# Pad tiles that bring TensorE's operands to one address modulo 256, and a start without GpSimd

## The chip, the cores and the metric

The kernel runs on one core of a Trainium2 chip. The metric is the device time of one execution in microseconds. Times of stretches come from one profiled execution and are counted from the start of its span.

## The reference

A two-layer diffusion backbone with D = 2048, 256 latent tokens and 256 context tokens, all in float32. Layer 0 mixes tokens with a windowed attention (16 heads of 128) that also sees the context; layer 1 mixes them with a gated MLP that multiplies 128-position chunks by a 128x128 matrix for each channel group. Each mixer is followed by a SwiGLU of inner width 5632. Shift, scale and gate of every sub-layer come from the conditioning vectors.

```python
for i in range(DEPTH):                       # DEPTH = 2
    sh1, sc1, g1, sh2, sc2, g2 = ada_params(c, ada_w[i], ada_b[i])   # silu(c) @ w + b
    a = modulate(h, sh1, sc1)
    y = na_mixer(a, ac, ...) if i == 0 else spatial_gating_mlp(a, ...)
    h = layer_norm(ALPHA * h + g1 * y, ...)
    h = layer_norm(ALPHA * h + g2 * swiglu(modulate(h, sh2, sc2), ffn_w_in[i], ffn_w_out[i]), ...)
```

## The kernel before

**Products.** Every large product is float32 split into two `float32r` halves, hi and lo, and made of three matmuls (`mm3`, L88 to L91): hi x hi, hi x lo, lo x hi. In `T.matmul(out, stationary, moving)` the second argument is loaded into the array by a weight load (PEld in the profile), the third streams through it; the profile names them `out<-moving,stationary`. One matmul streams 512 columns.

**Weights.** A queue of weight pieces of 128x1024 (`enqueue`, `prefetch`, `piece`) is loaded by SP into `raw` buffers and split by ScalarE (L94, hi) and VectorE (L95, lo). In layer 0's first half the split halves lie in three buffer pairs `hiA`, `loA` of the pool `outer`. From L553 on, five pairs are used in turn: of each five pieces three go to the `A` pairs in `outer` and two to the `B` pairs in the pool `main`. The last two pieces of some products go to `extra` tiles outside this turn.

```python
if pos["wide"] is not None and m % 5 > 2:
    pool, tag, bufs = pos["wide"], "B", 2
else:
    pool, tag, bufs = outer, "A", 3
```

**Input products** (`block_T`: the SwiGLU's gate and up, `pg` and `pu`, and the gated MLP's `gv` and `gu`) use tiles of the pool `main` as stationary operand: `f0h`, `f0l`, `m1h`, `m1l`, `f1h`, `f1l` (tags `acth`, `actl`). A piece gives 12 matmuls. **Output products** (`project_out`: `powo`, `pod`, `pogo`) use tiles `gh`, `gl` of `outer` (or `e`, also in `outer`). A piece gives 12 matmuls here too. In the attention half both operands lie in `outer`, `attnX`, `attnA` and `attnB`; a piece of `proj_v` gives 24 matmuls.

**Addresses.** A tile starts at a multiple of 32 bytes, and a pool's tags follow each other in the order of their first use; a pool opened later lies behind. In `outer` all tiles from `xT` on are whole multiples of 256 bytes, so `A`, `gh`, `gl`, `xT`, `ada` and the first tile of the pool behind, `ah` or `h`, have the same address modulo 256; call it r. In `main` follow `h` (16384 bytes), `ca` and `cb` (four of 64), `st` (two of 192): that is 128 past a multiple of 256, and `B`, `tmp`, `acth` and `actl` lie at r + 128. `mv` and `rs` (four of 32) bring `zt`, and the pools behind `main`, back to r. In the pool `gm` the 64 bytes of `bs` put `vv` at r + 64. The tiles `ah`, `al`, `kh`, `qh` and `v` of the attention half are at r.

**The start.** TensorE computes the first shift and scale columns with small matmuls (`dot`, L343: batches of 32 over a 1 MB load `ap`), a batch for each of two vectors, then `gather(kt)` (a ScalarE copy, L352, and two small matmuls against `sel`, L355; `sel` is a reduction of the identity, L314). `make_identity` builds the identity on GpSimd. After `gather(0)` two rows of the conditioning (`c_bc`, and `cc_bc`, which lies in `oT`) are each loaded to one partition by SP, spread over 128 partitions by GpSimd (`spread`, L81) and passed through SiLU by ScalarE (L382). From kt = 3 on VectorE uses them (L330). TensorE's order here is fixed by `pin`. Then the loop over kt: nine matmuls `kps`, the `dot` of kt + 2, twelve matmuls `vps`, `gather` of kt + 2, and from kt = 3 twelve matmuls `eps`.

**GpSimd later** zeroes the gate tiles (L171), spreads LayerNorm rows (L83) and sums the gates over partitions (`partition_all_reduce`, L192).

Of the kernel before, what the change touches and what calls it, by code (L numbers as in the profile page):

```python
# [11 lines left out]

F32 = mybir.dt.float32
F32R = mybir.dt.float32r
BF16 = mybir.dt.bfloat16
AF = mybir.ActivationFunctionType
# [4 lines left out]
P = 128  # L21
# [31 lines left out]
def hybrid_kernel(ctx: ExitStack, tc: tile.TileContext, i, out):  # L53
    nc = tc.nc
    V, S, T = nc.vector, nc.scalar, nc.tensor

    outer = ctx.enter_context(tc.tile_pool(name="outer", bufs=1))
# [3 lines left out]
    badj = outer.tile([P, 2, 6, KT], F32, tag="badj", name="badj")  # L61
    nc.scalar.dma_start(badj, i["ada_b_col"])
    ident = outer.tile([P, P], F32, tag="ident", name="ident")
    make_identity(nc, ident)
    eps_t = outer.tile([P, 1], F32, tag="eps", name="eps_t")
    nc.gpsimd.memset(eps_t, EPS)
    warm = outer.tile([P, 1], F32, tag="warm", name="warm")
# [13 lines left out]
    def spread(dst, src):  # L81
        nc.sync.dma_start(dst[0:1, :], src[None, :])
        nc.gpsimd.partition_broadcast(dst, dst[0:1, :])  # L83
# [194 lines left out]
    with tc.tile_pool(name="attnX", bufs=1) as px, ExitStack() as late:  # L278
# [21 lines left out]
        with tc.tile_pool(name="st", bufs=1) as st:  # L300
# [3 lines left out]
            def load_st(src, name, n):  # L304
# [2 lines left out]
                nc.sync.dma_start(r, src)  # L307
                return r

            c_pad = st.tile([P, KT, 32], F32, tag="cpad", name="c_pad")  # L310
            nc.gpsimd.memset(c_pad, 0.0)
            V.tensor_copy(c_pad[:, :, 0:2], c_col)
# [4 lines left out]
            vps = [stp_pool.tile([P, 512], F32, tag=f"v{b}", name=f"vps{b}") for b in range(4)]  # L317
            xt = {}
            c_bc = outer.tile([P, D], F32, tag="cbc", name="c_bc")
            cc_bc = oT[:, 0 : D // NT, :].rearrange("p a b -> p (a b)")  # L320
# [42 lines left out]
            def modulate(kt):  # L363
# [6 lines left out]
                    )  # L370
                split_into(ah[:, kt, :], al[:, kt, :], tmp)

            for kt in range(2):
                for t in range(2):
                    dot(kt, t)
                load_x(kt)
                prefetch(1)
                gather(kt)
                if kt == 0:
                    for n, bc in enumerate((c_bc, cc_bc)):  # L380
                        spread(bc, i["c_rows"][n])
                        S.activation(bc, bc, AF.Silu)  # L382
            modulate(0)
            for kt in range(KT):
                hi, lo = piece()
# [166 lines left out]
    main = ctx.enter_context(tc.tile_pool(name="main", bufs=1))  # L552
    pos["wide"] = main  # L553
    pos["bufs"] = 5
    h_t = main.tile([P, 2, D], F32, tag="h", name="h_t")
    nc.sync.dma_start(h_t, i["x_tok"])

    def act_tiles(name):
# [5 lines left out]
    def stats_tile(name):  # L564
        return main.tile([P, 2, NB, 6], F32, tag="st", name=f"st{name}", bufs=2)
# [96 lines left out]
    def project_out(kts, src, key, name, finish, extra, last=False):  # L662
        st = stats_tile(name)
        hold = LAST if last else HOLD
        for nh in range(2):
            if nh == 0:
                ps = [[acc_tile(f"po{name}{nh}{n}{b}") for b in range(2)] for n in range(2)]
            else:
                ps = [[s_tile(f"po{name}{nh}0{b}") for b in range(2)]]
                ps.append([acc_tile(f"po{name}{nh}1{b}") for b in range(2)])  # L670

            def products(kt, x, w, n, b):
                c, tb = slice(n * 512, (n + 1) * 512), slice(b * P, (b + 1) * P)
                mm3(ps[n][b], x[0][:, tb], x[1][:, tb], w[0][:, c], w[1][:, c], kt == 0, kt == kts - 1)

            def fetch(kt, n):
                xs = []
                for k in range(n):
                    at = None
                    if k >= START:  # L680
                        if k % 2 == 0:
                            e = outer.tile([P, 4, NT], F32R, tag="ada", name=f"e{name}{k}", bufs=ADA)
                        at = e[:, 2 * (k % 2), :], e[:, 2 * (k % 2) + 1, :]
                    xs.append(act_split(src(kt + k), f"{name}{nh}_{kt + k}", at))
                return xs, take(n)

            k0 = 0
            if nh == 1:
                xs, ws = fetch(0, START)
                for n in range(2):  # L690
                    for j in range(START):
                        for b in range(2):
                            products(j, xs[j], ws[j], n, b)
                preload_sqrt(st)
                k0 = START
            k1 = kts - hold if nh == 1 else kts
            for kt in range(k0, k1):
                if nh == 1 and kt == max(k1 - 9, k0):
                    pos["extra"] = extra()
                w = piece() if nh == 0 or kt < k1 - START else take(1)[0]  # L700
                x = act_split(src(kt), f"{name}{nh}_{kt}")
                for n in range(2):
                    for b in range(2):
                        products(kt, x, w, n, b)
                if nh == 0 or kt < k1 - QUIET:
                    tick()
            if nh == 0:
                need(key)
                g = gate[key]
                for n in range(2):  # L710
                    for b in range(2):
                        residual(ps[n][b], b, n, g, st, name)
            else:
                xs, ws = fetch(k1, hold)
                for b in range(2):
                    for n in range(2):
                        for j in range(hold):
                            products(k1 + j, xs[j], ws[j], n, b)
                        with tc.high_priority(AHEAD):
                            residual(ps[n][b], b, 2 + n, g, st, name)  # L720
                    if not last:
                        with tc.high_priority(AHEAD):
                            finish(b, st)
                if last:
                    for b in range(2):
                        finish(b, st)
# [25 lines left out]
    def ffn(layer, m, key, name, finish, free, last=False):  # L752
# [41 lines left out]
    m = Modulated(0, 0, SH2, SC2, "f0")  # L794
    free = ExitStack()
    pw = free.enter_context(tc.tile_pool(name="pw", bufs=1))
    project_out(
        KT, lambda k: oT[:, k, :], (0, G1), "wo", m.first,
        lambda: pw.tile([P, 4, 1024], F32R, tag="w", name="extra_o"),
# [21 lines left out]
    pg = free.enter_context(tc.tile_pool(name="gm", bufs=1))  # L821
    ws = pg.tile([P, NH, P], F32, tag="ws", name="ws")
    nc.sync.dma_start(ws, i["w_s"])
    bs = pg.tile([P, NH], F32, tag="bs", name="bs")
    nc.sync.dma_start(bs, i["b_s"])
    vv = pg.tile([P, 2, D], F32, tag="vv", name="vv")
    st = stats_tile("v")
    for nb in range(NB):
        ps = [acc_tile(f"gv{nb}{b}") for b in range(2)]
        block_T(m, ps, nb == 0)  # L830
        for b in range(2):
            sl = slice(nb * 512, (nb + 1) * 512)
# [106 lines left out]
def lay_out(x, c, ctx, c_ctx, ada_w, ada_b, ln_g, ln_b, na_w_qkv, na_w_o, na_rpb,  # L939
            gm_w_in, gm_ln_g, gm_ln_b, gm_w_s, gm_b_s, gm_w_out, ffn_w_in, ffn_w_out):  # L940
    a = {}
    x, ctx = x[0], ctx[0]
    rows = np.stack([c[0], c_ctx])
    a["c_rows"] = rows
    a["c_col"] = rows.reshape(2, KT, P).transpose(2, 1, 0)
    xc = np.concatenate([x, ctx], 0)
    a["xcT"] = xc.T.reshape(KT, P, 512)
    a["x_tok"] = x.reshape(2, P, D).transpose(1, 0, 2)
    a["ada_b_col"] = ada_b.reshape(2, 6, KT, P).transpose(3, 0, 1, 2)
    a["ada_b_row"] = ada_b.reshape(2, 6, D)  # L950
    g4, b4 = ln_g.reshape(4, D), ln_b.reshape(4, D)
    a["ln_row"] = np.stack([g4, b4], 1)
    a["ln_col"] = a["ln_row"].reshape(4, 2, KT, P).transpose(3, 0, 1, 2)
    aw = ada_w.reshape(2, D, 6, D)
    dot = np.empty((len(DOT), P, D), np.float32)
    for (layer, t, nt), n in DOT.items():
        dot[n] = aw[layer, :, t, nt * P : (nt + 1) * P].T
    a["ada_t"] = dot
    a["ada_g"] = np.concatenate(
        [aw[layer, :, t, :].reshape(KT, P, D) for layer in range(2) for t in (G1, G2)], 0  # L960
    )
    a["ada_p"] = np.stack(
        [[aw[0, :, t, kt * P : (kt + 1) * P].reshape(KT, P, P).transpose(1, 0, 2).reshape(P, 2048)
          for t in (SC1, SH1)] for kt in range(KT)]
    )
    a["ada_s"] = np.stack([aw[0, :, SH1, kt * P : (kt + 1) * P].T for kt in range(DVE0, KT)])
    wq, wk, wv = (na_w_qkv[0][:, n * D : (n + 1) * D] for n in range(3))
    w0 = np.concatenate([wk[:, : HK0 * P], wv[:, :512]], 1)
    a["w_kv0"] = w0.reshape(KT, P, W0)

    a["w_q"] = heads(wq)
    a["w_k"] = heads(wk)[HK0:]
    a["w_v"] = blocks_512(wv)[1:]
    a["bias"] = bias_layout(na_rpb[0])
    a["w_o"] = halves(na_w_o[0])
    parts = ffn_w_in.reshape(2, D, 2, DFF)
    a["w_in_t"] = np.stack([[blocks_512(parts[n, :, p]) for p in range(2)] for n in range(2)])
    a["w_out"] = np.stack([halves(w) for w in ffn_w_out])
    a["w_gin"] = blocks_512(gm_w_in[0])
    a["w_gout"] = halves(gm_w_out[0])  # L980
    a["gm_row"] = np.stack([gm_ln_g[0], gm_ln_b[0]])
    a["w_s"] = gm_w_s[0].transpose(2, 0, 1)
    a["b_s"] = gm_b_s[0].T
    return {k: np.ascontiguousarray(v) for k, v in a.items()}
# [17 lines left out]
```

## Time and profile before

| | before |
|---|---|
| median of 3 runs (lowest to highest) | 2493.1 us (2491.81 to 2497.22) |
| profiled execution: its time, its span | 2484.16 us, 2482.4 us |
| TensorE busy in the span | 2409.0 us, 97% |
| VectorE, ScalarE, GpSimd busy | 1754.9, 1118.9, 110.5 us |

A busy TensorE is not a TensorE at its best: a matmul counts as busy from its start to its modelled end, and matmuls overlap. How fast it goes is read from one start to the next.

### The profile page before, as it was taken

The numbers are of one execution on the slowest core, as the hardware profiler recorded it, in microseconds if no ns is written. First come the engines' busy times: TensorE is split into PE (matmuls) and PEld (weight loads), VectorE is DVE, ScalarE is ACT, GpSimd is POOL, SyncE is SP. The second block draws the span as 40 slices with busy tenths as digits, with TensorE's granted clock in tenths as the row PEclk, the third lists the DMA queues.
The fourth block names the chain that finished last, engine by engine and source line by source line (L and its number), as shares of the span: only waits on it lengthen the run. The fifth ranks groups of instructions, "written<-read, shape, count | busy, mean of one in ns | idle before, by whom it ended". The sixth has DMA issues, their size and how long they took to land. (4 is left out here: it accounts for less than half of the span.)

```text
span 2482.4 us, 31276 instructions
## 1 busy us (share of the span) xinstructions
PE 2409.0 (97%) x11574; PEld 1976.3 (80%) x11574; DVE 1754.9 (71%) x2159; ACT 1118.9 (45%) x1534; POOL 110.5 (4%) x56
## 2 busy tenths in 40 slices
PE   6999899999999999999999999999999999999998
PEld 5787788888778888888888778777888888888886
DVE  3878877776877676666778778778755555566666
ACT  3344434345554444444455554446544444445453
POOL 0000200000010020000000020020100000020000
PEclk8999999999999999999999999999999999999999
DMA  8977787777568878888888767765676666666563
GB/s 328 347 258 253 243 285 269 268 269 240 184 225 299 283 272 287 280 285 291 283 290 278 255 211 259 255 205 184 214 228 224 218 222 226 220 196 190 174 208 131
DMA packets 167394, 610.57 MB, mean 246 GB/s; under 512 B 18916, under 2 KB 21284, under 8 KB 162884
## 3 DMA queue, kind: packets, MB, share of 16 engines
q1 hardware_dynamic: 120888, 440.64, 53.5%
q10 hardware_dynamic: 46224, 167.89, 19.6%
q8 instruction: 90, 1.47, 0.2%
q14 instruction: 64, 0.52, 0.1%
q0 software_dynamic: 128, 0.03, 0.0%
HBM read 606.40 MB, written 2.10 MB: 245 GB/s over the span
## 5 line engine op out<-in xcount | busy, mean ns | idle before, releaser
L94 ACT CAST hwf<-rwf 128x1024 fp32r<-128x1024 f32 x320 | 335.7, 1049 | 505.6 <-PE pu L91 228.5
L95 DVE TENSOR_TENSOR lwf<-rwf,hwf 128x1024 fp32r<-128x1024 f32 x320 | 405.5, 1276 | 194.2 <-ACT hwf L94 193.3
L153 DVE SCALAR_TENSOR_TENSOR ad<-ad,c_bc 128x1024 f32<-128x1024 f32 x192 | 234.0, 1222 | 169.8 <-DMA ad<-in_ada_t 169.2
L91 PE MATMUL pod<-hwd,gld 128*128 128x512 f32 x684 | 267.9, 392 | 0.7 <-DVE gld L95 0.7
L89 PE MATMUL pod<-hwd,ghd 128*128 128x512 f32 x684 | 268.2, 392 | 0.0
L90 PE MATMUL pod<-lwd,ghd 128*128 128x512 f32 x684 | 267.8, 392 | 0.0
L95 DVE TENSOR_TENSOR lwd<-rwd,hwd 128x1024 fp32r<-128x1024 f32 x172 | 211.5, 1231 | 52.4 <-ACT hwd L94 51.9
L177 DVE SCALAR_TENSOR_TENSOR gate<-ag,c_col,gate 128x1024 f32<-128x1024 f32 x128 | 164.3, 1287 | 108.8 <-DMA ag<-in_ada_g 108.5
L94 ACT CAST hwd<-rwd 128x1024 fp32r<-128x1024 f32 x172 | 179.9, 1046 | 26.2 <-PE pu L91 17.2
L91 PEld LDWEIGHTS pod<-hwd,gld 128*128 128x128 f32 x684 | 128.3, 188 | 29.6 <-DVE gld L95 1.1
L90 PEld LDWEIGHTS pod<-lwd,ghd 128*128 128x128 f32 x684 | 128.4, 188 | 28.5
L89 PEld LDWEIGHTS pod<-hwd,ghd 128*128 128x128 f32 x684 | 128.4, 188 | 28.5
L89 PE MATMUL pg<-hwf,f0h 128*128 128x512 f32 x320 | 127.5, 398 | 0.0
L89 PE MATMUL pg<-hwf,f1h 128*128 128x512 f32 x320 | 127.5, 398 | 0.0
L91 PE MATMUL pg<-hwf,f1l 128*128 128x512 f32 x320 | 125.8, 393 | 0.0
L91 PE MATMUL pg<-hwf,f0l 128*128 128x512 f32 x320 | 125.8, 393 | 0.0
L90 PE MATMUL pg<-lwf,f0h 128*128 128x512 f32 x320 | 125.7, 393 | 0.0
L90 PE MATMUL pg<-lwf,f1h 128*128 128x512 f32 x320 | 125.7, 393 | 0.0
L91 PE MATMUL pu<-hwf,f0l 128*128 128x512 f32 x320 | 125.7, 393 | 0.0
L91 PE MATMUL pu<-hwf,f1l 128*128 128x512 f32 x320 | 125.7, 393 | 0.0
L90 PE MATMUL pu<-lwf,f0h 128*128 128x512 f32 x320 | 125.7, 393 | 0.0
L89 PE MATMUL pu<-hwf,f1h 128*128 128x512 f32 x320 | 125.7, 393 | 0.0
(341 smaller groups left out, 5341.9 us busy)
## 6 DMA issues: line engine op xcount, KB each, us to landing
rwf<-in_w_in_t SPq DMA_DIRECT2D x320, 512.0 KB
ad<-in_ada_t ACTq DMA_DIRECT2D x192, 512.0 KB
rwd<-in_w_out SPq DMA_DIRECT2D x176, 512.0 KB
ag<-in_ada_g ACTq DMA_DIRECT2D x128, 512.0 KB
rwg<-in_w_gin SPq DMA_DIRECT2D x64, 512.0 KB
ap<-in_ada_p SPq DMA_DIRECT2D x19, 1024.0 KB
rwq<-in_w_q SPq DMA_DIRECT2D x32, 512.0 KB
rwo<-in_w_o SPq DMA_DIRECT2D x32, 512.0 KB
```

What stands on the lines that cost most here:

```text
L89: keep(T.matmul(ps, sh, mh, start=first, stop=False))
L90: keep(T.matmul(ps, sh, ml, start=False, stop=False))
L91: keep(T.matmul(ps, sl, mh, start=False, stop=last))
L94: S.copy(hi, src)
L95: V.tensor_tensor(lo, src, hi.bitcast(F32), ALU.subtract)
L153: V.scalar_tensor_tensor(r, r, 1.0, c_bc[:, half * 1024 : (half + 1) * 1024], ALU.mult, ALU.mult, accum_out=o[:, nt : nt + 1],)
L177: V.scalar_tensor_tensor(g, loaded.pop(key), c_col[:, kt, 0:1], g, ALU.mult, ALU.add)
```

## The change

A tile of 32 floats (128 bytes) is put behind `h` in `main`, one of 128 bytes ahead of the `extra_o` tile in `pw`, and one of 64 bytes behind `bs` in `gm`. Nothing reads or writes them. The identity comes from DRAM over ScalarE's DMA queue instead of `make_identity`. The two conditioning rows are loaded, over the same queue, as two tiles of 2 partitions x 1024 in `loA` buffers; `pick` (in a `gh` buffer) holds a row of the identity's first two rows spread over 128 columns, and `widen` multiplies it with the rows, so that each of 4 matmuls gives 512 columns of one conditioning row on all 128 partitions, in the PSUM tiles `vps`. ScalarE takes SiLU from there. `widen(0)` stands ahead of the first `dot`, `widen(1)` behind `gather(0)`. The SP loads, GpSimd broadcasts and 2048-wide SiLUs of before are gone.

```diff
     ident = outer.tile([P, P], F32, tag="ident", name="ident")
-    make_identity(nc, ident)
+    nc.scalar.dma_start(ident, i["ident"])
...
+            c_row = [outer.tile([2, 1024], F32, tag="loA", name=f"c_row{e}", bufs=3) for e in range(2)]
+            for e in range(2):
+                nc.scalar.dma_start(c_row[e], i["c_rows"][:, e * 1024 : (e + 1) * 1024])
+            pick = outer.tile([2, 2, P], F32, tag="gh", name="pick", bufs=4)
+            for n in range(2):
+                V.tensor_copy(pick[:, n, :], ident[0:2, n : n + 1].to_broadcast([2, P]))
...
+            def widen(n, bc):
+                for q in range(4):
+                    sl = slice(q * 512, (q + 1) * 512)
+                    cs = slice(q % 2 * 512, q % 2 * 512 + 512)
+                    pin(T.matmul(vps[q], pick[:, n, :], c_row[q // 2][:, cs], start=True, stop=True))
+                    S.activation(bc[:, sl], vps[q], AF.Silu)
+
+            widen(0, c_bc)
             for kt in range(2):
                 for t in range(2):
                     dot(kt, t)
...
                 gather(kt)
                 if kt == 0:
-                    for n, bc in enumerate((c_bc, cc_bc)):
-                        spread(bc, i["c_rows"][n])
-                        S.activation(bc, bc, AF.Silu)
+                    widen(1, cc_bc)
...
     h_t = main.tile([P, 2, D], F32, tag="h", name="h_t")
+    main.tile([P, 32], F32, tag="pad", name="pad_main")
...
     pw = free.enter_context(tc.tile_pool(name="pw", bufs=1))
+    pw.tile([P, 32], F32, tag="pad", name="pad_pw")
...
     nc.sync.dma_start(bs, i["b_s"])
+    pg.tile([P, 16], F32, tag="pad", name="pad_gm")
     vv = pg.tile([P, 2, D], F32, tag="vv", name="vv")
...
+    a["ident"] = np.eye(P, dtype=np.float32)
```

## Rows read from the trace of the kernel before

**Rows 1.** The page's first part: busy us of each engine (share of the span) and its instructions.

```profile
PE 2409.0 (97%) x11574; PEld 1976.3 (80%) x11574; DVE 1754.9 (71%) x2159; ACT 1118.9 (45%) x1534; POOL 110.5 (4%) x56
```

**Rows 2.** Busy time by stretch. Columns: from:to, length, busy us and instruction count of PE, PEld, DVE, ACT and POOL, granted clock of PE, mean busy share of the DMA engines, GB/s.

```profile
72.00:150.00 78.00, 78.00 (x593) 62.11 (x592) 66.22 (x88) 30.19 (x54) 0.00 (x0) 1.00 0.91 331
150.00:600.00 450.00, 429.19 (x2366) 371.63 (x2365) 347.10 (x518) 190.19 (x309) 15.43 (x3) 0.98 0.78 261
600.00:1750.00 1150.00, 1130.71 (x4978) 915.21 (x4977) 864.64 (x1054) 555.97 (x745) 61.57 (x33) 1.00 0.76 256
1750.00:2450.00 700.00, 700.00 (x3086) 571.00 (x3085) 420.60 (x420) 314.45 (x385) 27.85 (x10) 1.00 0.65 210
```

**Rows 3.** What TensorE waited for over the span, one of the two longest: engine, line, releaser, us in total, times, longest.

```profile
PE aps L355 <- ACT row L352: 11.4, 2, 10.2
```

**Rows 4.** Timeline of TensorE in an input product of layer 1 (start us, us, engine line op out<-moving,stationary). Between the first and the second row lie three pieces (36 matmuls), between the second and the third two pieces (24).

```profile
1854.32 0.40 PE L89 MATMUL pu<-hwf,f1h 128*128 128x512 f32 x1
...
1862.71 0.39 PE L89 MATMUL pu<-hwf,f1h 128*128 128x512 f32 x1
...
1868.17 0.40 PE L89 MATMUL pg<-hwf,f1h 128*128 128x512 f32 x1
```

**Rows 5.** The same for an output product of layer 1. Between the first and the second row lie two pieces (24 matmuls), between the second and the third three (36).

```profile
2382.29 0.40 PE L89 MATMUL pod<-hwd,ghd 128*128 128x512 f32 x1
...
2387.88 0.39 PE L89 MATMUL pod<-hwd,ghd 128*128 128x512 f32 x1
...
2396.06 0.40 PE L89 MATMUL pod<-hwd,ghd 128*128 128x512 f32 x1
```

**Rows 6.** The same for one piece of the attention's value product (24 matmuls from the first row to the second).

```profile
455.91 0.39 PE L89 MATMUL vps<-hwv,ah 128*128 128x512 f32 x1
...
461.35 0.39 PE L89 MATMUL vps<-hwv,ah 128*128 128x512 f32 x1
```

**Rows 7.** Timeline of TensorE: the first and the last of the 512-column matmuls whose two operands differ modulo 256 and whose next matmul starts within 260 ns (4068; with the others 4152).

```profile
589.47 0.40 PE L89 MATMUL powo<-hwo,ghwo 128*128 128x512 f32 x1
...
2466.71 0.39 PE L91 MATMUL pod<-hwd,gld 128*128 128x512 f32 x1
```

**Rows 8.** The first and the last of those whose operands agree and whose next matmul starts within 260 ns (5218).

```profile
36.38 0.40 PE L90 MATMUL vps<-lkv,ah 128*128 128x512 f32 x1
...
2469.90 0.39 PE L90 MATMUL pod<-extra,ed 128*128 128x512 f32 x1
```

**Rows 9.** Groups of VectorE's L95 by operands: out<-in, count, busy us, mean ns, idle before and its releaser. In the first the inputs differ modulo 256 (r and r + 128), in the second they agree.

```profile
L95 DVE TENSOR_TENSOR f0l<-zsf,f0h 128x512 fp32r<-128x512 f32 x8 | 5.5, 686 | 2.2 <-ACT f0h L94 2.2
L95 DVE TENSOR_TENSOR vl<-v,vh 128x512 fp32r<-128x512 f32 x16 | 10.9, 684 | 0.4 <-ACT vh L94 0.4
```

**Rows 10.** Timeline of the start, all engines (in brackets the idle time before it on its engine, and what ended it).

```profile
2.94 0.27 DVE L70 TENSOR_SCALAR badj<-badj 128x32 f32<-128x32 f32 x2 [2.94 <-DMA badj<-in_ada_b_col]
...
6.76 1.93 PE L343 MATMUL aps<-ap,c_pad 128*32 128x128 f32 x32 [6.76 <-DMA ap<-in_ada_p]
...
11.84 0.28 POOL masks.py:199 TENSOR_SCALAR_AFFINE_SELECT ident<-ident 128x128 f32<-128x128 f32 x1 [10.41 <-issue]
...
12.47 0.98 PE L355 MATMUL aps<-sel,row 128*128 128x2 f32 x4 [0.91 <-DVE sel L314]
...
21.71 2.30 POOL L83 PARTITION_BROADCAST c_bc<-c_bc  x1 [9.59 <-issue]
...
24.05 1.91 ACT L382 ACTIVATE c_bc<-c_bc 128x2048 f32<-128x2048 f32 x1 [8.37 <-POOL c_bc L83]
26.22 1.91 ACT L382 ACTIVATE oT<-oT 128x2048 f32<-128x2048 f32 x1 [0.27 <-POOL oT L83]
28.04 0.35 ACT L352 COPY row<-aps 128x256 f32<-128x256 f32 x1
...
28.45 1.01 PE L355 MATMUL aps<-sel,row 128*128 128x2 f32 x4 [10.25 <-ACT row L352]
...
29.32 0.78 PE L89 MATMUL kps<-ah,hkv 128*128 128x512 f32 x1
...
33.44 2.68 PE L343 MATMUL aps<-ap,c_pad 128*32 128x128 f32 x64
...
36.05 0.50 PE L89 MATMUL vps<-hkv,ah 128*128 128x512 f32 x1
```

**Rows 11.** The same at kt = 2, from its first `kps` to its first `vps`.

```profile
45.64 0.39 PE L89 MATMUL kps<-ah,hkv 128*128 128x512 f32 x1
...
47.77 1.08 PE L343 MATMUL aps<-ap,c_pad 128*32 128x128 f32 x32
```

**Rows 12.** Timeline of TensorE: a float32 matmul of 256 columns, which leaves two records, and the next start on the engine.

```profile
1576.41 0.60 PE L846 MATMUL sp<-vv,ws 128*128 128x256 f32 x2
1576.93 0.66 PE L851 MATMUL uvt<-ident,u 128*128 128x128 f32 x4
```

**Rows 13.** ScalarE's SiLU of 512 columns from PSUM, as a group (columns as in Rows 9).

```profile
L778 ACT ACTIVATE sg<-pg 128x512 f32<-128x512 f32 x44 | 26.2, 598 | 24.0 <-PE pg L91 24.0
```

**Rows 14.** Timeline of GpSimd: the first of four sums of a gate over partitions.

```profile
268.27 12.78 POOL L192 PARTITION_ALL_REDUCE gate<-gate  x1 [111.52 <-DVE gate L177]
```

**Rows 15.** Busy time around the first and the last of these sums (columns as in Rows 2).

```profile
250.00:300.00 50.00, 41.31 (x256) 37.24 (x255) 41.29 (x50) 23.79 (x40) 12.78 (x1) 0.93 0.72 239
2150.00:2200.00 50.00, 50.00 (x223) 40.65 (x222) 32.77 (x22) 19.80 (x21) 12.78 (x1) 1.00 0.59 192
```

More of the change, by code (lines that the diff above doesn't have):

```diff
@@ L10 @@
 from concourse._compat import with_exitstack
-from concourse.masks import make_identity
 F32 = mybir.dt.float32
```

## The prediction

> **What bounds the kernel now.** First the busy times: TensorE is busy for 2409.0 of 2482.4 us, VectorE for 1754.9 [rows 1]. Then busy time by stretch: from 1750 to 2450 TensorE is busy for 700.00 of 700 us, between 600 and 1750 it lacks 19 us, in the attention half 21 of 450, and the loop over kt is full from 72 to 150 [rows 2]. So nearly all of the span is the row of matmuls, and there are two things to gain: what the matmuls take from start to start, and the start, where TensorE's longest single wait lies (10.2 of 11.4 us behind ScalarE's `row`) [rows 3]. The timeline shows what busy time hides. In an input product three pieces of 12 matmuls take 8.39 us, or 233.1 ns a matmul, and the next two 5.46 us, 227.5 ns [rows 4]. In an output product two pieces take 5.59 us, 232.9 ns, and the next three 8.18, 227.2 ns [rows 5]. Three and two is the turn of the buffers: three `A` pieces at address r, two `B` pieces at r + 128. In the input product, with its stationary operand at r + 128, `A` is the slow one; in the output product, with it at r, `B` is. Neither buffer is slow as such; a pair that differs modulo 256 is. In the attention half both are at r, and a piece takes 5.44 us, 226.7 ns [rows 6].
>
> **The pads: count.** An input product of 512 columns has 16 x 2 x 3 = 96 matmuls; there are 22 per SwiGLU and 8 in the gated MLP, 52 in all, so 4992, of which `A` is three in five. The output products have 24 for each of 44 + 44 + 16 + 16 row blocks, 2880, of which `B` is two in five. That would be 2995 + 1152; with the `extra` pieces, which don't take part in the turn, the program's order laid beside the trace has 4152 that differ [rows 7].
>
> **The pads: price.** In the clean stretches a pair that differs costs 5.6 to 5.7 ns more [rows 4, 5]. Over every interval under 260 ns it is less: the 4068 that differ have a mean of 232.9 ns [rows 7], the 5218 that agree 227.7 [rows 8]; the rest of the spread comes with both. I take 5.2 ns, since that mean holds what stays: 4152 x 5.2 = 21.6 us. Bounds: 24 us by the clean stretches, 16 if a quarter of it is given back in the stretches that wait anyway.
>
> After the change everything in `main` behind `h` moves on by 128 bytes: `B`, `f0h` and their like come to r, as `A` and `gh` are, and `extra_o` and `vv` are put back to r by their own pads. So all pairs agree. What leaves r are `gTb`, `sg`, `zt` and `ws`. `gTb` and `zt` are read by VectorE and ScalarE, and VectorE's L95 takes 686 ns with inputs that differ and 684 with inputs that agree [rows 9]: nothing. `ws` differs from `vv` before and after, and `sg` from the identity too.
>
> [...]
>
> **The start: what goes.** GpSimd's `affine_select` ends at 12.12 and delays `gather(0)` by 0.91 us. The first broadcast starts at 21.71, the SiLUs wait for it in ScalarE's order at 24.05 and 26.22, and behind them the copy for `gather(1)`, at 28.04, so TensorE stands from 18.20 to 28.45 [rows 10]. It then works at the lower of its two clock levels: nine `kps` and 64 small matmuls take from 29.32 to 36.05, 6.73 us [rows 10]; at full clock nine `kps` take 2.13 and 32 small ones 1.08 [rows 11], so 4.3. That is 2.4 us more.
>
> **What comes.** Eight float32 matmuls of 512 columns. The nearest row: 256 columns take 0.52 us to the next start at full clock [rows 12], so 1.0 us for 512, 2.0 at half. The identity and the rows come over ScalarE's queue; `badj`, the first there, has landed at 2.94 [rows 10]. Three DMAs behind it and two tiny copies on VectorE let me put the first `widen` matmul at 5. The first batches ran at 1.93 us instead of 1.08, so TensorE starts at half clock [rows 10, 11]; after 29.32 it had risen by 36, some 6 us of unbroken work. With a rise at 11: three matmuls until 11, one until 12, two batches of 1.08 until 14.2 (before, both had been worked by 12.47, so their loads are there), `gather(0)` with its 0.35 us copy and 0.98 of matmuls until 15.7, `widen(1)` 4.0 until 19.7, two batches until 21.9, `gather(1)`, 1.28 us from copy to `kps` before and 1.0 at full clock, until 22.9. `kps` starts 6.4 us earlier than at 29.32, and 2.4 are saved behind it: 8.8. The eight SiLUs of 598 ns [rows 13] lie beside the matmuls on ScalarE, ahead of the copy that waited; were they in its way, they would cost up to 2.4 a row. The two `c_row` tiles hold two `loA` buffers until 19.7, and the second split is needed behind 29; nothing. The `ap` loads are freed up to 4 us later, as `widen(0)` stands ahead of them on TensorE, and SP's queue waits for that; the loop has room (DMA share 0.91 and VectorE 66 of 78 us, TensorE 78 of 78 [rows 2]), but the first two rounds have little, and I take off 0.8: 8 us. Bounds: a clock that rises early and `widen` at the rate of its columns alone give 10.5; half clock throughout gives 5 + 8 + 3.9 + 1.5 + 8 + 3.9 + 1.3 = 31.6 against 29.3, a loss of 2.
>
> **Sum.** 21.6 + 8 = 29.6 us. The profiled execution took 2484.2 (1.8 around the span), so 2454.6; the median of the runs stands 8.9 above it, so 2463.5.
>
> **Rivals.** *Addresses are worth nothing*: weight load and moving operand don't meet, and the slow pieces are slow for another reason that the pads leave in place, or an unused tile takes no room. Then 8 us: 2485. Against it stands the crossing [rows 4, 5]; nothing in the trace speaks for it. Chance 0.05. [...] *The start gives nothing*: `widen` runs at half clock and the loads come late, so only the pads count: 2471.5. For it: TensorE is cold there, and 8 long matmuls stand in its fixed order. Against: the hole it fills is 10.25 us. Chance 0.12. [...] Chance 0.03. The forecast itself has 0.8.
>
> **The numbers.** Predicted 2463. The lower end takes both upper bounds (24 + 10.5: 2458.6) and a spread of the runs of 5 below; the upper one pads at 16 and a start at -1 (2478). This leaves out the first and third rival and some of the second's tail. A change under 0.2%, 5 us, can't be told from none; all cases but the third rival, and the first with a start that fails too, lie beyond it on the faster side: 0.95, 0.03, 0.02.
>
> **What would show it.** In the timeline every piece of `pu`, `pg` and `pod` should take 2.72 to 2.74 us, with no three-and-two; one that still takes 2.80 shows an operand off r. The first `kps` should start at 20 to 24 at full clock, with no GpSimd work before 150. VectorE's L95 means should stay at some 1220 ns. The prediction is wrong if slow pieces stay, if TensorE waits for VectorE or DMA in 600 to 2450 where it had none, or if the first `kps` comes behind 28.

## The result, and the profile after

The changed kernel takes 2464.15 us at the median of 4 runs (2461.48 to 2466.86); the kernel before, measured beside it, 2492.45 (4 runs, one more than in the table). The ratio is 0.9895, 95% interval 0.9872 to 0.9918: 28 us faster, against the 30 forecast. Its profiled execution has a span of 2462.5 us (2464.24 with what lies around it), 19.9 less than the one of before, which was 8 us quicker than its own median. The steps behind the number did not all hold, and a second comparison came out smaller.

The page's first part, busy us and instructions of each engine; [rows 1] answers to it.

```profile
PE 2394.4 (97%) x11590; PEld 1982.1 (80%) x11590; DVE 1754.3 (71%) x2161; ACT 1120.8 (46%) x1540; POOL 108.0 (4%) x52
```

Busy time by stretch, kernel after (from:to, length, busy us and count of PE, PEld, DVE, ACT, POOL, granted clock, DMA share, GB/s), as in [rows 2]:

```profile
0.00:72.00 72.00, 62.18 (x494) 44.16 (x494) 34.12 (x54) 25.89 (x45) 0.76 (x6) 0.93 0.93 342
72.00:150.00 78.00, 78.00 (x592) 62.27 (x592) 66.24 (x87) 30.12 (x53) 0.00 (x0) 1.00 0.89 322
150.00:600.00 450.00, 426.07 (x2347) 369.88 (x2346) 343.86 (x512) 187.26 (x304) 15.22 (x3) 0.98 0.78 259
600.00:1750.00 1150.00, 1127.60 (x5029) 925.77 (x5028) 873.23 (x1065) 563.86 (x755) 67.52 (x35) 1.00 0.77 258
1750.00:2430.00 680.00, 680.00 (x3045) 563.32 (x3044) 412.31 (x410) 309.82 (x379) 24.49 (x8) 1.00 0.66 214
```

TensorE still sets the end. In the same 1150 us behind 600 it now works off 5029 matmuls, where it was 4978: they are shorter on average. But it also stands idle longer, 22.4 us there and 23.9 in the attention half, 46.3 together, where before it was 19.3 and 20.8, together 40.1 [rows 2].

Timeline of TensorE, kernel after (start us, us, engine line op out<-moving,stationary): an input product of layer 1 and an output product, as in [rows 4, 5]. Between the first and the second row of each lie 24 matmuls, between the second and the third 36.

```profile
1828.94 0.39 PE L89 MATMUL pg<-lwf,f1h 128*128 128x512 f32 x1
...
1834.38 0.39 PE L89 MATMUL pu<-lwf,f1h 128*128 128x512 f32 x1
...
1842.54 0.39 PE L89 MATMUL pu<-lwf,f1h 128*128 128x512 f32 x1
...
2362.21 0.39 PE L89 MATMUL pod<-lwd,ghd 128*128 128x512 f32 x1
...
2367.65 0.39 PE L89 MATMUL pod<-lwd,ghd 128*128 128x512 f32 x1
...
2375.81 0.39 PE L89 MATMUL pod<-lwd,ghd 128*128 128x512 f32 x1
```

5.44 and 8.16 us in both, 226.7 ns a matmul: the three-and-two is gone, and the pace is that of the attention half [rows 6].

Timeline of the start, kernel after, as in [rows 10, 11]:

```profile
7.04 0.35 DVE L314 COPY pick<-ident 2x128 f32<-2x128 f32 x2 [3.86 <-DMA ident<-in_ident]
7.31 7.19 PE L382 MATMUL vps<-c_row,pick 2*128 2x512 f32 x8 [7.31 <-DVE pick L314]
14.43 3.64 PE L348 MATMUL aps<-ap,c_pad 128*32 128x128 f32 x64
18.56 0.74 PE L360 MATMUL aps<-sel,row 128*128 128x2 f32 x4 [0.49 <-ACT row L357]
19.23 4.21 PE L382 MATMUL vps<-c_row,pick 2*128 2x512 f32 x8
23.37 3.64 PE L348 MATMUL aps<-ap,c_pad 128*32 128x128 f32 x64
28.38 0.77 PE L88 MATMUL kps<-ah,hkv 128*128 128x512 f32 x1
32.49 1.95 PE L348 MATMUL aps<-ap,c_pad 128*32 128x128 f32 x64
34.38 0.50 PE L88 MATMUL vps<-hkv,ah 128*128 128x512 f32 x1
```

The hole of 10 us is filled, but with slow matmuls. `widen(0)` takes 7.19 us, `widen(1)` 4.21 (four matmuls of two records each), the first two pairs of `aps` batches 3.64 each and the one at 32.49 only 1.95. So TensorE works at a low level until some 18.9, at a higher one until 22.3, and low again until 32.5. The granted clock of a stretch shows the fall at 22.3, from 1.00 to 0.50 (columns as above):

```profile
19.00:22.00 3.00, 3.00 (x10) 1.52 (x10) 0.35 (x2) 2.21 (x5) 0.00 (x0) 1.00 0.95 350
23.00:32.00 9.00, 8.51 (x78) 6.62 (x77) 2.57 (x6) 4.25 (x7) 0.00 (x0) 0.50 0.90 311
```

Ahead of 18.9 the profile lists 1.00 as well (8 to 18), though two batches take the same 3.64 us there as at 0.50 behind 23: the level of the first 19 us, here and in the starts below, is read from the times of the matmuls alone.

The first `kps` comes at 28.38 where it was 29.32 [rows 10], and the first `vps` at 34.38 where it was 36.05: the start brings 1.7 us in this execution. A first `kps` behind 28 is one of the signs that the prediction gave for being wrong. TensorE's longest waits are now these (engine, line, releaser, us in total, times, longest); [rows 3] has the wait that left the list:

```profile
PE pt L531 <- ACT p L521: 19.0, 7, 6.9
PE vps L382 <- DVE pick L314: 7.3, 1, 7.3
```

### The profile page after: what moved, and what is told of

The parts are those of the page before. It is cut to its first block, busy times and chain, and to the rows that moved or that the text cites. A ratio compares the mean times of both kernels' runs of the same rounds, so it can differ in the third digit from the quotient of the medians.

```text
span 2462.5 us, 31307 instructions
## 1 busy us (share of the span) xinstructions
PE 2394.4 (97%) x11590; PEld 1982.1 (80%) x11590; DVE 1754.3 (71%) x2161; ACT 1120.8 (46%) x1540; POOL 108.0 (4%) x52
## 5 line engine op out<-in xcount | busy, mean ns | idle before, releaser
L94 DVE TENSOR_TENSOR lwf<-rwf,hwf 128x1024 fp32r<-128x1024 f32 x320 | 404.6, 1278 | 172.3 <-ACT hwf L93 171.6
L94 DVE TENSOR_TENSOR lwd<-rwd,hwd 128x1024 fp32r<-128x1024 f32 x172 | 212.0, 1233 | 54.9 <-ACT hwd L93 54.8
L88 PE MATMUL pu<-hwf,f0h 128*128 128x512 f32 x320 | 124.5, 389 | 0.0
L89 PE MATMUL pu<-lwf,f1h 128*128 128x512 f32 x320 | 124.5, 389 | 0.0
```

Of the source, the lines that this page charges most:

```text
L88: keep(T.matmul(ps, sh, mh, start=first, stop=False))
L89: keep(T.matmul(ps, sh, ml, start=False, stop=False))
L94: V.tensor_tensor(lo, src, hi.bitcast(F32), ALU.subtract)
```

## The experiments

Each ratio is against the kernel before on the same chip, with its 95% interval; that kernel's medians were 2487.34 us beside the first four, 2487.22 beside the next four and 2490.01 beside the last three.

**The pads alone.** The kernel before with the three pad tiles:

```
     h_t = main.tile([P, 2, D], F32, tag="h", name="h_t")
+    main.tile([P, 32], F32, tag="pad", name="pad_main")
...
+    pw.tile([P, 32], F32, tag="pad", name="pad_pw")
...
+    pg.tile([P, 16], F32, tag="pad", name="pad_gm")
```

> The kernel before with the three pad tiles alone; the start is as it was. Theory A (the pads give nearly all of the gain; the profile of the changed kernel shows 226.9 ns between the starts of 512-column matmuls in place of 232.9 and 227.7): 25 to 28 us less than before, ratio 0.989 to 0.990, all pieces of 12 matmuls at 2.72 us, the first kps at 29.3 as before. Rival B (the pads give the 21.6 us that was predicted and the rest is the start): ratio 0.9913, 2471 us.

2468.03 us, ratio 0.9922 (0.9903 to 0.994): 19.3 us. The page's first part, and two stretches of it:

```profile
PE 2385.6 (97%) x11574; PEld 1979.3 (80%) x11574; DVE 1752.1 (71%) x2159; ACT 1121.2 (46%) x1534; POOL 110.3 (4%) x56
```

```profile
150.00:600.00 450.00, 429.62 (x2364) 372.98 (x2363) 346.75 (x518) 190.19 (x309) 15.42 (x3) 0.98 0.77 261
600.00:1750.00 1150.00, 1125.07 (x5010) 923.31 (x5009) 868.51 (x1061) 561.87 (x750) 64.47 (x35) 0.99 0.76 257
```

With the same 11574 matmuls TensorE is busy 23.4 us less than before [rows 1], but the span is only 18.4 shorter (2464.0): it waits 5.0 us more. The two stretches show it, 20.4 + 24.9 = 45.3 us idle where before it was 40.1 [rows 2]. Each figure is from one execution, and the repeats further down differ by 4 to 6 us with no edit at all, so that the pads cause these waits is not shown. The addresses are worth most of the change, and by the median of the runs the pads lie nearer to the 21.6 us of the sum than to theory A's 25 to 28; by TensorE's own busy time they lie between the two.

**The start alone.** The changed kernel without the pads (`pad_main`, `pad_pw`, `pad_gm` taken out), measured twice:

```
-    main.tile([P, 32], F32, tag="pad", name="pad_main")
...
-    pw.tile([P, 32], F32, tag="pad", name="pad_pw")
...
-    pg.tile([P, 16], F32, tag="pad", name="pad_gm")
```

> The changed kernel without its three pads: only the identity from DRAM and the rows spread by TensorE are left. Theory A (the start gives 1.7 us at the first vps product, as in the profile of the changed kernel, and the attention half gives it back, since VectorE waits there for the loads of the modulation weights whatever TensorE does): ratio 0.998 to 1.001. Rival B (the start gives the 6 to 8 us that was predicted, and the profiled execution was an unlucky one): ratio 0.997 to 0.9965. Three pieces at 2.80 us and two at 2.73 must be back in the SwiGLU.

2484.35 us, 0.9988 (0.9973 to 1.0002). And again, beside the last two kernels below:

> The start of the change alone, on two rows, a second time, to stand beside the 128 rows without pads. Both theories: 0.9975 to 1.0, with the clock at its lower level until some 28 us.

2485.59 us, 0.9989 (0.9973 to 1.0005). By the medians that is 3.0 and 4.4 us, and both intervals reach 1: it can't be told from none. The forecast had 8 for it. In the two profiled executions the first `vps` starts at 32.80 and 34.67, 3.3 and 1.4 us ahead of before [rows 10].

**A difference of 64 bytes.** The changed kernel with other pads, so that everything in `main` stands at r + 64 where the changed kernel has r:

```
-    main.tile([P, 32], F32, tag="pad", name="pad_main")
+    main.tile([P, 48], F32, tag="pad", name="pad_main")
...
-    pw.tile([P, 32], F32, tag="pad", name="pad_pw")
+    pw.tile([P, 16], F32, tag="pad", name="pad_pw")
...
-    pg.tile([P, 16], F32, tag="pad", name="pad_gm")
```

> The changed kernel with the pad in main 192 bytes long (and the pads behind it cut so that extra_o and vv stay at r): everything in main lies at r + 64, so the same pairs as before differ, by 64 bytes in place of 128. Theory A (what counts is equal or not modulo 256): about 4150 matmuls slow again, the turn of three slow pieces and two fast ones in the SwiGLU, some 5 to 6 ns each, ratio 0.997 to 1.000 of before. Rival B (only a difference of 128 collides): as the changed kernel, ratio 0.9895.

2485.81 us, 0.9981 (0.9963 to 0.9998): no gain beyond that of the start. The input product of layer 1 (TensorE's timeline; 36 matmuls from the first row to the second, 24 to the third):

```profile
1836.13 0.39 PE L89 MATMUL pg<-lwf,f1h 128*128 128x512 f32 x1
...
1844.53 0.40 PE L89 MATMUL pu<-lwf,f1h 128*128 128x512 f32 x1
...
1849.99 0.39 PE L89 MATMUL pu<-lwf,f1h 128*128 128x512 f32 x1
```

8.40 us is 233.3 ns a matmul, 5.46 us 227.5: in this product a difference of 64 costs as much as one of 128 did [rows 4]. With the program's order and addresses laid beside the trace, the pairs that differ take 233.3 ns in the input products (2969 of them) and only 229.7 in the output products, where it is the moving operand that lies 64 higher (1091); those that agree 228.1. In the changed kernel 4049 pairs lie 256 bytes apart modulo 512 and take 226.9 ns: of the differences tried, 256 alone costs nothing. And since the tiles of `main` move in the kernel with r + 64 too, it is the equal address that gains, not the move.

**The broadcast on 128 rows.** The changed kernel, with `c_row` and `pick` on 128 partitions; the 126 added rows of `c_row` are zeros, so the sums are the same, and so is the number of columns:

```
-c_row = [outer.tile([2, 1024], F32, tag="loA", ...) for e in range(2)]
+c_row = [outer.tile([P, 1024], F32, tag="loA", ...) for e in range(2)]
 for e in range(2):
-    nc.scalar.dma_start(c_row[e], ...)
+    V.memset(c_row[e], 0.0)
+    nc.scalar.dma_start(c_row[e][0:2, :], ...)
-pick = outer.tile([2, 2, P], F32, tag="gh", ...)
+pick = outer.tile([P, 2, P], F32, tag="gh", ...)
 for n in range(2):
-    V.tensor_copy(pick[:, n, :], ident[0:2, n : n + 1].to_broadcast([2, P]))
+    V.tensor_copy(pick[:, n, :], ident[:, n : n + 1].to_broadcast([P, P]))
```

> The changed kernel with c_row and pick on all 128 partitions: c_row is set to zero but for its first two rows, so widen streams 128 rows in place of 2 and gives the same result. Theory A (the clock stayed at its lower level, and fell again behind widen(1), because widen kept only 2 of 128 rows busy): the clock rises during or behind widen(0) and stays up; the first 64 small matmuls take 2.2 in place of 3.64 us, the nine kps 2.1 in place of 4.1, and the first vps starts at about 29 in place of 34.4. Rival B (it is the time or the pauses alone): the same steps as in the changed kernel, first vps at 34.4. In both the end moves less than the start if the attention half gives the gain back.

2456.12 us, 0.9863 (0.984 to 0.9885). TensorE's timeline at the start:

```profile
7.40 5.43 PE L383 MATMUL vps<-c_row,pick 128*128 128x512 f32 x8 [7.40 <-DMA c_row<-in_c_rows]
12.76 1.95 PE L349 MATMUL aps<-ap,c_pad 128*32 128x128 f32 x64
...
15.67 3.68 PE L383 MATMUL vps<-c_row,pick 128*128 128x512 f32 x8
19.28 1.96 PE L349 MATMUL aps<-ap,c_pad 128*32 128x128 f32 x64
...
22.19 0.48 PE L88 MATMUL kps<-ah,hkv 128*128 128x512 f32 x1
...
26.32 0.50 PE L88 MATMUL vps<-hkv,ah 128*128 128x512 f32 x1
```

The clock, by these times, rises at 10.9, inside `widen(0)` (its weight loads take 0.34 us before, 0.20 from 10.94 on), and stays: the two pairs of batches take 1.95 and 1.96, and the first `vps` comes at 26.32, 9.7 us ahead of before and 8.1 ahead of the changed kernel. On TensorE only the rows are other; VectorE has the two `memset`s more, and the first `widen` matmul starts at 7.40 where it was 7.31.

**Both once more, side by side.** The changed kernel and the one with 128 rows, with no further edit:

> The changed kernel once more, beside the next three on one chip, so that the starts can be compared. Theory A (the clock's level at the start is worth some 8 us at 80 us, of which the attention half gives back part): ratio 0.989 to 0.991, slower than the kernel with 128 rows. Rival B (the attention half gives all of a better start back, and the lower time of the kernel with 128 rows was another chip): the same ratio as that kernel within 0.001.

> The kernel with widen on all 128 rows once more, on the chip of the others. Theory A: 4 to 8 us (0.0015 to 0.003) faster than the changed kernel, clock up from about 11 us on. Rival B: the same as the changed kernel.

The changed kernel took 2464.96 us, 0.9914 (0.9899 to 0.9929), the one with 128 rows 2452.58, 0.986 (0.9846 to 0.9875). TensorE's timeline at the start, first the changed kernel, then the one with 128 rows:

```profile
7.15 7.19 PE L382 MATMUL vps<-c_row,pick 2*128 2x512 f32 x8 [7.15 <-DVE pick L314]
...
19.35 7.19 PE L382 MATMUL vps<-c_row,pick 2*128 2x512 f32 x8
...
31.06 0.48 PE L88 MATMUL kps<-ah,hkv 128*128 128x512 f32 x1
...
35.20 0.50 PE L88 MATMUL vps<-hkv,ah 128*128 128x512 f32 x1
```

```profile
7.12 6.39 PE L383 MATMUL vps<-c_row,pick 128*128 128x512 f32 x8 [7.12 <-DVE pick L315]
...
27.01 0.50 PE L88 MATMUL vps<-hkv,ah 128*128 128x512 f32 x1
```

With two rows both `widen` now run at the low level, 7.19 us each, and the first `kps` comes at 31.06, later than in the kernel before (29.32 [rows 10]): on two rows `widen(1)` took 4.21 us in one execution of this kernel and 7.19 in the other. The median with 128 rows is 12.4 us lower, more than theory A had, of which the start shows 8.2 (first `vps` at 27.01 against 35.20); the other 4 are no more than the waits differ between executions, told below. In this comparison the gain of the change itself is 22 us, not 28.

**No broadcast on TensorE.** The changed kernel with the rows spread over the partitions by two DMAs on SP's queue, at the place of `widen(1)`, and no `widen`:

```
-widen(0, c_bc)
...
-    widen(1, cc_bc)
+    for n, bc in enumerate((c_bc, cc_bc)):
+        nc.sync.dma_start(bc, i["c_rows"][n : n + 1, :].to_broadcast([P, D]))
+        S.activation(bc, bc, AF.Silu)
```

> The changed kernel without widen: each conditioning row is spread by a DMA that reads it for all 128 partitions (2 MB more of loads on SP's queue ahead of ap10), and ScalarE takes SiLU of 2048 columns as in the kernel before. Theory A (what is left of the start is TensorE's clock and the time of its 16 widen records): TensorE has nothing to spread, but pauses for the loads, so that its clock is low; first vps at 29 to 32, between the changed kernel (34.4) and the one with 128 rows (26.3), ratio between theirs. Rival B (the loads set the start): the 2 MB push the start back by 5 us, first vps at 36 or later.

2463.91 us, 0.9903 (0.9887 to 0.9918): as the change. TensorE's timeline:

```profile
7.35 4.00 PE L342 MATMUL aps<-ap,c_pad 128*32 128x128 f32 x64 [7.35 <-DVE c_pad L311]
...
18.74 1.94 PE L342 MATMUL aps<-ap,c_pad 128*32 128x128 f32 x32 [5.90 <-DMA ap<-in_ada_p]
...
23.88 0.49 PE L88 MATMUL kps<-ah,hkv 128*128 128x512 f32 x1
...
31.84 0.80 PE L88 MATMUL vps<-hkv,ah 128*128 128x512 f32 x1
```

The first `kps` comes at 23.88, but with a hole of 5.90 us ahead of it, where the next `ap` block waits behind the rows, and two of 1.3 us behind it; the granted clock falls again (0.50 from 30 to 36), and the first `vps` takes 0.80 us at 31.84, where with 128 rows it takes 0.50. From the first `kps` to the first `vps` it takes 7.96 us, with 128 rows 4.13: of the 3.8 us between them 2.7 are these two waits (the profile puts the first down to VectorE's `lkv`, the second to a load of `ap`), and most of the rest is the second batch, which takes 1.94 us where the first took 1.08. Taking the broadcast off TensorE is not enough if the loads come late for it.

**Work moved out of the attention half.** The kernel with 128 rows, and the tasks of layer 1's `SH1` moved from the attention half to the first SwiGLU:

```
     add_tasks(0, G1, SH2, SC2)
-    add_tasks(1, SH1)
...
-    add_tasks(1, SC1, SH2, SC2)
+    add_tasks(1, SH1, SC1, SH2, SC2)
```

> The kernel with widen on all 128 rows, and the 32 tasks of layer 1's first shift moved from the attention half to the tasks beside layer 0's SwiGLU (16 MB of loads less in the attention half). Theory A (VectorE's waits for these loads, some 80 us in the attention half, hold up the softmax and so TensorE, and there the start's gain is given back): VectorE's waits for ad and ag between 160 and 590 fall by a quarter or more, TensorE's for p from 17 to below 10 us, and the start's 9.7 us are still there at 600; ratio 2 to 5 thousandths below that of the kernel with 128 rows. Rival B (the loads don't hold up TensorE): TensorE's waits in the attention half and the ratio stay as they are, or the SwiGLU gets slower by the loads moved there.

2447.23 us, 0.9839 (0.9822 to 0.9857), the lowest median of the kernels tried. But not as expected. VectorE's waits for its loads between 160 and 590, first the kernel with 128 rows (its first run), then this one:

```profile
DVE ad L152 <- DMA ad<-in_ada_t: 62.7, 37, 5.5
DVE gate L176 <- DMA ag<-in_ada_g: 17.5, 12, 2.5
```

```profile
DVE ad L152 <- DMA ad<-in_ada_t: 58.2, 35, 6.7
DVE gate L176 <- DMA ag<-in_ada_g: 19.7, 12, 3.4
```

They hardly fell, though VectorE has 313.2 us of work from 150 to 600 where the repeat with 128 rows has 345.8; and neither did TensorE's idle time from 150 to 600 (19.8 us, where the repeat with 128 rows has 19.4). The intervals of this kernel and of that repeat overlap. That the move is what helps is not shown.

**The start on 128 rows, without the pads.** To see what a start at the higher level is worth by itself, the three pads are taken out of the kernel with 128 rows:

```
-    main.tile([P, 32], F32, tag="pad", name="pad_main")
...
-    pw.tile([P, 32], F32, tag="pad", name="pad_pw")
...
-    pg.tile([P, 16], F32, tag="pad", name="pad_gm")
```

> The new start with the rows on 128 partitions (126 of them zeros), without the pads. It asks what the start is worth by itself once the clock has risen. Theory A: the clock decides the start, and what the start brings reaches the end but for some us that the attention half takes back: full clock from 10.9 to 12.6 as in the padded kernels with 128 rows, 9 to 10 us ahead of before at 80 us, and a ratio of 0.9955 to 0.9975 (6 to 11 us), so at least 4 us less than the start on two rows measured beside it. Rival B: the attention half takes back all of it, and the 12 us between the padded kernels with 2 and with 128 rows came from how the pads and the start fall together: the same 9 to 10 us at 80 us, but a ratio within 0.001 of the start on two rows.

2478.52 us, 0.9953 (0.9932 to 0.9974), beside 2485.59 for two rows. TensorE's first `kps` and `vps`, first here, then with two rows:

```profile
23.73 0.48 PE L88 MATMUL kps<-ah,hkv 128*128 128x512 f32 x1
...
27.86 0.50 PE L88 MATMUL vps<-hkv,ah 128*128 128x512 f32 x1
```

```profile
28.74 0.77 PE L88 MATMUL kps<-ah,hkv 128*128 128x512 f32 x1
...
34.67 0.50 PE L88 MATMUL vps<-hkv,ah 128*128 128x512 f32 x1
```

6.8 us earlier at the first `vps`, 7.1 at the end by the medians; against the kernel before 8.2 and 11.5. What the start gains reaches the end, and theory A holds, with a ratio just below the 0.9955 to 0.9975 that it gave. (At the first `vps` it is 8.2 us ahead, not 9 to 10: the clock rose later in this execution, in the last part of `widen(0)`, which took 6.65 us.)

**The identity first.** The kernel with 128 rows, with two DMAs of ScalarE's queue exchanged:

```
+    nc.scalar.dma_start(ident, i["ident"])
     nc.scalar.dma_start(badj, i["ada_b_col"])
-    nc.scalar.dma_start(ident, i["ident"])
```

> The change with the rows on 128 partitions, and the identity's DMA ahead of the adaLN bias on ScalarE's queue instead of behind it. It asks why the identity landed at 7.0 and not at 4.5. Theory A: its place in the queue sets its landing, behind the bias and beside the 1 MB loads of SP's queue, which begin at 1.2: landed by 4.5, the first broadcast matmul at 4.5 to 5.5 instead of 7.4, the first kps 2 to 3 us earlier than 22.2, and 1 to 3 us off the whole, which the times can hardly tell. Rival B: the DMA engines are shared with the 1 MB loads whatever its place, and it lands at 6 to 7 again.

2456.18 us, 0.9884 (0.9853 to 0.9914), no gain over 128 rows. Timeline of the start:

```profile
2.93 0.29 DVE L315 COPY pick<-ident 128x128 f32<-128x128 f32 x2
...
7.19 0.27 DVE L69 TENSOR_SCALAR badj<-badj 128x32 f32<-128x32 f32 x2 [3.90 <-DMA badj<-in_ada_b_col]
...
7.53 2.05 PE L383 MATMUL vps<-c_row,pick 128*128 128x512 f32 x2 [7.53 <-DVE badj L69]
```

The identity, now first, is read at 2.93; `badj`, now second, at 7.19. In both orders the first of the two is read at 2.9, as theory A has it. But the first of the queue is also issued at 0.74, ahead of SP's first 1 MB loads (1.19), and the second beside them (1.19), so whether its place in the queue or the loads decide was not told apart. The first matmul stays at 7.53, where 5 was expected: it now follows the second DMA's reader on VectorE (by the trace; the third and fourth DMA, the rows, were not told apart from it).

## Why the prediction was right, and where its steps were not

**Count and price of the pads: right in the mechanism, and in the time by two errors that go against each other.** The forecast had 4152 x 5.2 = 21.6 us; the pads alone gave 19.3. The price is higher: 232.9 ns [rows 7] became 226.9, so 6.0, and 4152 x 6.0 = 24.9; that is above the upper bound taken, 24. Nor did the pairs that agreed stay at 227.7 ns, on which the 5.2 rests: the 3670 of them in input and output products had 227.7 and have 226.9 as well, some 3 us that the sum left out. Against this TensorE waits some 5 us more in the stretches that waited already, which the lower bound had named and the sum had not put a price on. A piece of the changed kernel's input and output products takes 2.72 us (12 matmuls at 226.9 ns).

**What hides and what leaves r: right.** VectorE's `lwf` and `lwd` take 1278 and 1233 ns (1276 and 1231 before), its `f0l` 688 [rows 9].

**The start: mis-sized, 8 us forecast, 3.0 and 4.4 measured, not told from none.** The prediction's own sign of this came true: the first `kps` behind 28, at 28.38 and, in the repeat, 31.06. Two terms of its sum failed. *First, "put the first `widen` matmul at 5"*: it began at 7.31, since the identity, second on ScalarE's queue, was read only at 7.04; that `badj`, first there, had landed at 2.94 [rows 10] said nothing for the second. *Second, "with a rise at 11"*: the rise was derived from 6 us of unbroken work by matmuls of 128 rows, and put to matmuls of two rows. With two rows the low level stayed through 7.19 us of `widen(0)` and 3.64 of batches and came back at 22.3, in `widen(1)`, or, in the repeat, stayed through both `widen`; with 128 rows it rose at 10.9 and 12.6, inside `widen(0)`, and stayed. There the end of the forecast's chain is met: `kps` at 22.2 and 22.9, where 22.9 was forecast, 9 to 10 us gained at the first `vps`, where 8.8 were. In part that is luck: the chain begins 2 us later than put, and its two `widen` take 5.4 to 6.4 and 3.7 us, where 7 and 4 were put. The rows shown don't say why two rows and 128 differ. With 128 rows the rise came 3.5 and 5.5 us behind the first matmul; with two rows it came only behind 10.8 us of matmuls, and the granted clock fell again, while matmuls on two rows ran, to 0.50. The bound of 10.5 us has `widen` at the rate of its columns alone; no run shows that rate, the quickest four matmuls took 3.68 us.

**The sum.** In the profiled pair it closes: 24.9 us by the pads, 1.7 by the start, less 6.2 more idle time from 150 to 1750 (46.3 less 40.1), makes 20.4, and the spans differ by 19.9; the 3 us of the agreeing pairs would put it at 23.4, so it closes to some 4 us. By medians the parts alone give 19.3 and 3.0 to 4.4, 22 to 24 us; the whole gave 28 and, in the second comparison, 22. So the time fell on the forecast, but part of that is the luck of one comparison: the forecast's ratio, 2463.0 to 2493.1 or 0.988, lies inside the first interval and below the second. A gain of 22 to 28 is what is shown, 30 was claimed.

**The rivals.** *Addresses are worth nothing* fell (0.9922 for the pads alone): a pair of operands that differ by 128 bytes costs TensorE 6 ns a matmul (232.9 [rows 7] became 226.9). *The start gives nothing*, with "`widen` runs at half clock and the loads come late", had the right mechanism, both of its halves; it had 0.12, and deserved more. The hole of 10.25 us that spoke against it was filled, but by work that took almost as long. *The third rival*, a slower kernel by way of GpSimd's gate sums, did not come: the first gate sum still begins as soon as its gate is there, at 266.72, lasts 12.78 us as before [rows 14], and TensorE is busy for 42.13 of the 50 us around it (41.31 in [rows 15]). VectorE is not held up for the whole of a sum: during that one an `lwk` split of 128x512 takes 7.15 us, where the shortest takes 0.68, and VectorE's other instructions run at their usual pace (a `kl` split of the same size takes 0.68); during the second sum four `lwf` splits take 13.55 us, where four take 5.1 elsewhere. So these two sums cost VectorE some 6 to 8 us each. *TensorE's waits* from 600 to 2450, the prediction's third sign, are all on engines, none on a DMA; TensorE stands idle for 22.4 us up to 1750 and for none behind, where before it was 19.3 and none; two waits for VectorE, 1.5 us for `sg` and 1.7 ahead of `ztm` for `h_t`, are not among those of before. So this sign came true too, in a small way.

**What stays open.** The same kernel's idle time between 150 and 1750 differs from one profiled execution to the next: 46.3 and 42.3 us for the changed kernel, 46.9 and 40.6 for the one with 128 rows, the longest part of it at TensorE's wait `pt` for ScalarE's `p` (11.4 to 19.0 us over all kernels), in the attention half, where VectorE waits some 80 us for its loads in each of them. What sets it in an execution was not found; moving `SH1` did not change it. It limits every reading from a single execution to about 5 us. Nor do the runs show why unequal addresses cost time, only that they do.

## What to carry to other kernels

Where TensorE is full and pieces of one product take two paces in a pattern that follows the buffers, compare the byte addresses of moving and stationary operand modulo 256, and make them equal by a pad tile: 6 ns of 233 a matmul of 512 columns here, for no instruction. Work that is put into TensorE's hole at the start is judged by the pace of the batches behind it, not by the busy share: here 128 rows, all but two of them zeros, held the two-batch time at 1.95 us, where two rows had 3.64 and a granted clock of 0.50. And the landing of a small DMA can't be taken from its forerunner's: here the second of two came 4 us later.

## What the runs showed of the hardware

- The cost of unequal addresses: 232.9 ns at 128 bytes apart (4068 matmuls, 43 of them 64 apart), 233.3 at 64 with the stationary operand the higher one, 229.7 with the moving one, 226.9 at 0 and at 256 (start to start, 512 columns, input and output products).
- Four float32 matmuls of 512 columns on two rows took 7.19 us at the low level and, on 128 rows at the high one, 3.68: some 0.9 us each, where 1.0 had been estimated. With two rows the granted clock fell from 1.00 to 0.50 at 22.3 while they ran.
- Of two small DMAs issued 0.45 us apart on ScalarE's queue, the second beside the first 1 MB loads on SP's, the first was read at 2.9 us and the second at 6.5 to 7.2, whichever of the two tiles it was.
